# Products of quarters in two shared PSUM tiles: five additions on VectorE for seven, the first quarter read by ScalarE

## The chip, the cores and the metric

The kernel runs on 1 core of a Trainium2 chip. The metric is the device time of one execution in microseconds (us); the median of three runs is the time before. One more execution was taken with the hardware profiler; durations and order of events below come from it.

## The reference

One layer of an encoder block with two parallel mixers, on x of 1024 tokens by 1024 channels, all in float32:

```python
h = rmsnorm(x, norm_gain)
z = jnp.einsum('bsd,de->bse', h, w_in)
q, k, v, gate_a, u_in, v_in, gate_b, g_merge = jnp.split(z, IN_SPLITS, axis=-1)
...
attn = block_attention(q, k, v) * jax.nn.silu(gate_a)
y_a = jnp.einsum('bse,ed->bsd', attn, w_proj_attn)
...
gm = u * v_mix.reshape(B, S, GMLP_WIDTH) * jax.nn.silu(gate_b)
y_b = jnp.einsum('bse,ed->bsd', gm, w_proj_gmlp)
g = jax.nn.sigmoid(g_merge.reshape(B, S, N_BRANCHES, D_MODEL) + b_merge)
y = g[:, :, 0, :] * y_a + g[:, :, 1, :] * y_b
return x + jnp.einsum('bsd,de->bse', y, w_out)
```

A final rmsnorm follows. The change concerns two of these products: g_merge (1024 tokens by 1024 channels by 2 x 1024 columns) and y_a (1024 tokens by 512 by 1024 columns).

## The kernel before

Everything is transposed: channels lie on the 128 partitions, tokens along the free dimension, in two halves of 512 (`H(0)`, `H(1)`). Each float32 operand is split into a high and a low part, and each block product is three matmuls, high by high, high by low, low by high (`mm3`, lines 171 to 174). The stages follow each other: projections of k, v and q, attention (mixed with the other projections), the products for y_b (`proj_b`), then the stage of the change, then the output projection (`out_mm`, tiles out0 to out7) with the residual and the final norm.

In the stage of the change a two by two block product is made from seven products of half-size quarters instead of eight (a Strassen scheme in Winograd's form). `pair(dt, ...)` makes one block row of the gates, ga and gb, for dt of 0 to 7; `proj_pair(i, ...)` makes two block rows of y_a, for i of 0 to 3. Both call `seven`. The sums and differences of the input (forms, written xf for the gates and gf, gk for y_a) are made once in `make_forms`; the sums of the weights in `sums` and line 703. A weight quarter is scaled and cut into its high part on ACT and its low part on DVE (`split16`, lines 680 and 681, tiles wg; `split`, lines 110 and 116, tiles wp). The weights rotate through three buffers, so the parts for a product can be made when the product three before it is done. The seven products are called 11, 21, T2, T3, T1, 22 and T4 by the form that they read. A gate product is 12 matmuls, a projection product 6.

PSUM tiles of the tag "S" are two banks wide (128 x 1024 float32), and there are three of them. Before the change each product takes one and uses its first bank. c is the list of output halves: c[0][0] and c[0][1] are the halves of ga, c[1][0] and c[1][1] those of gb.

`unit_scale` gives the scale of a pair's weights: four squares on ACT (line 814, tiles gsq), a small matmul on PE (usg), a sum on DVE, a power on POOL (scg), a reciprocal on DVE. When a pair and its y_a are ready, `merge` (lines 835 to 837) makes y from them with three 1024-wide instructions, and `split_y` and `out_weight` cut y and the output weights (yhl, who, wo) for the output stage.

The order on each engine is not the order of the code: the scheduler of the tile framework orders instructions by a simulated timeline, with their order in the code as priority, and then sets semaphore waits. Each engine goes through its own list in order, so an instruction that waits holds all that stand behind it. `MORDER` gives the priority of the steps: w0 g0 w1 g1 w2 A a0 g2 w3 g3 w4 a1 g4 and so on, where w is `pair_weights`, g is `pair` and a is `proj_pair`.

Of the kernel before, what the change touches and what calls it, by code (L numbers as in the profile page):

```python
# [12 lines left out]
AF = mybir.ActivationFunctionType  # L13
# [17 lines left out]
def hybrid_block_kernel(  # L31
# [11 lines left out]
    act, dve, pool, pe = nc.scalar, nc.vector, nc.gpsimd, nc.tensor  # L43
# [9 lines left out]
    def t4(tag, name, dt=F32, shape=(P, 1024)):  # L53
        return sb.tile(list(shape), dt, tag=tag, bufs=BUFS[tag], name=name)

    def t2(name, dt=F32):
        return sb.tile([P, 512], dt, tag="t2", bufs=4, name=name)
# [10 lines left out]
    def const(shape, name, dt=F32):  # L68
        return sb.tile(shape, dt, tag=name, bufs=1, name=name)

    def ps_s(name):
        return ps.tile([P, 1024], F32, tag="S", bufs=3, name=name)
# [10 lines left out]
    def H(h):  # L83
        return slice(512 * h, 512 * h + 512)

    def C(c):
        return slice(128 * c, 128 * c + 128)
# [26 lines left out]
    def split(hi, lo, raw, eng, eng_lo=dve):  # L114
        hi_part(eng, hi, raw)
        eng_lo.tensor_tensor(out=lo, in0=raw, in1=hi if hi.dtype == F16 else hi.bitcast(F32), op=ALU.subtract)  # L116

    def load_w(i, half, tag="wraw", bufs=4):
        raw = sb.tile([P, 512], F32, tag=tag, bufs=bufs, name=f"wraw{i}{half}")
        nc.sync.dma_start(out=raw, in_=wall[i, :, H(half)])  # L120
        return raw
# [22 lines left out]
    def load_x(dt):  # L144
        raw = t4("T16", f"xraw{dt}")
        hi = t4("xh", f"xh{dt}", F32R)
        lo = t4("xl", f"xl{dt}", F32R)
        cuts = [slice(0, 256), slice(256, 512), H(1)] if dt == 0 else [slice(0, 1024)]
        for i, r in enumerate(cuts):
            nc.sync.dma_start(out=raw[:, r], in_=xT[C(dt), r])  # L150
            if dt == 0 and i == 0:
                nc.scalar.dma_start(out=cs, in_=cst[:, 0:C_BSP])
            if dt == 0 and i != 1:
                first_w(i // 2)
        for r in cuts:
            act.activation(hi[:, r], raw[:, r], AF.Copy, scale=gain[:, dt:dt + 1])
            dve.scalar_tensor_tensor(out=lo[:, r], in0=raw[:, r], scalar=gain[:, dt:dt + 1], in1=hi[:, r].bitcast(F32),
                                     op0=ALU.mult, op1=ALU.subtract)
        xh.append(hi)
        xl.append(lo)  # L160
        return raw
# [6 lines left out]
        nc.sync.dma_start(out=xn, in_=x[C(tt), :])  # L168
        act.activation(xn, xn, AF.Square, accum_out=ssx[:, tt:tt + 1])

    def mm3(o, ah, al, bh, bl, start, stop):
        pe.matmul(o, ah, bh, start=start, stop=False)  # L172
        pe.matmul(o, ah, bl, start=False, stop=False)  # L173
        pe.matmul(o, al, bh, start=False, stop=stop)  # L174

    kvs = [ps_s(f"kv{b}") for b in range(2)]
    kvb = [s[:, H(h)] for s in kvs for h in range(2)]
    for i in range(4):
        for j in range(2):
            dt = 2 * i + j  # L180
            if dt == 0:
                wh = sb.tile([P, 512], F32R, tag="wh", bufs=3, name="whk0")
                wl = sb.tile([P, 512], F32R, tag="wl", bufs=3, name="wlk0")
                wr = sb.tile([P, 512], F32, tag="wraw", bufs=4, name="wrawk0")
            raw = load_x(dt)
            if i == 0:
                r = slice(256 * j, 256 * j + 256)
                split(wh[:, r], wl[:, r], wr[:, r], act)
            elif j == 0:
                wh, wl = stream_w(W_KV + i // 2, i % 2, act)  # L190
            r = slice(256 * j, 256 * j + 256)
            for tt in range(NT):
                o = kvb[tt // 2][:, 256 * (tt % 2):256 * (tt % 2) + 256]
                mm3(o, xh[dt][:, C(tt)], xl[dt][:, C(tt)], wh[:, r], wl[:, r],
                    dt == 0 and tt % 2 == 0, dt == 7 and tt % 2 == 1)
# [48 lines left out]
    bmh = const([P, 16], "bmh")  # L244
# [10 lines left out]
    for h in range(2):  # L255
        raw = sb.tile([P, 512], F32, tag="wraw", bufs=4, name=f"wspr{h}")
# [37 lines left out]
    def spatial(c, vhl):  # L294
        vh, vl = vhl
        pt = ps_s(f"sp{c}")
        for t in range(4):
            r = slice(256 * t, 256 * t + 256)
            mm3(pt[:, r], vh[:, C(t)], vl[:, C(t)], wsh[:, r], wsl[:, r], True, True)
        p3 = pt.rearrange("p (k i) -> p k i", k=4)  # L300
        for g2 in range(2):
            rows = slice(64 * g2, 64 * g2 + 64)
            act.copy(vm[rows, :, C(c)], p3[rows, :, C(g2)])
# [130 lines left out]
    for t2k in range(4):  # L434
# [5 lines left out]
        for v in range(2):  # L440
            for half in range(2):
                dst = kT[64 * half:64 * half + 64, 2 * v:2 * v + 2, 256 * t2k:256 * t2k + 256]
# [235 lines left out]
    def split16(hi, lo, raw, sc, how):  # L678
        if how == "dve":
            act.activation(hi, raw, AF.Copy, scale=sc[:, 0:1])  # L680
            dve.scalar_tensor_tensor(out=lo, in0=raw, scalar=sc[:, 0:1], in1=hi, op0=ALU.mult, op1=ALU.subtract)
        else:
            act.activation(raw, raw, AF.Copy, scale=sc[:, 0:1])
            split(hi, lo, raw, pool if how == "pool" else act, pool)

    def seven(name, n, w, B, c, weights):

        def product(key, raw):
            hi, lo = weights(key, raw)
            bank = ps_s(f"{name}{key}")[:, H(0)]  # L690
            for j in range(n):
                mm3(bank, hi[:, C(j)], lo[:, C(j)], *B[key][j], j == 0, j == n - 1)
            return bank

        def add(dst, bank, other):
            dve.tensor_tensor(out=dst, in0=bank, in1=other, op=ALU.add)

        a11, a12, a21, a22, s1, s2 = w
        p1 = t2(f"p1{name}")
        act.copy(p1, product("11", a11))  # L700
        add(c[0][0], product("21", a12), p1)
        add(c[0][1], product("T2", s2), p1)
        dve.tensor_tensor(out=s2, in0=a12, in1=s2, op=ALU.subtract)
        add(c[1][0], product("T3", a21), c[0][1])
        o = product("T1", s1)
        add(c[1][1], o, c[1][0])
        add(c[0][1], o, c[0][1])
        add(c[0][1], product("22", s2), c[0][1])
        yield
        add(c[1][0], product("T4", a22), c[1][0])  # L710
        yield

    def sums(a11, a12, a21, a22, s1, s2):
        dve.tensor_tensor(out=s1, in0=a21, in1=a22, op=ALU.add)
        dve.tensor_tensor(out=s2, in0=s1, in1=a11, op=ALU.subtract)
        dve.tensor_tensor(out=a21, in0=a11, in1=a21, op=ALU.subtract)
        return a11, a12, a21, a22, s1, s2
# [63 lines left out]
    for dt in range(8):  # L781
        proj_b(dt)
        if dt in XCS:
            j = XCS.index(dt)
# [4 lines left out]
    def halves_of(t):  # L789
        return [t[:, H(0)], t[:, H(1)]]  # L790

    def proj_pair(i, b, G, dst):
        r0, r1 = load_w(W_PROJ + 2 * i, b), load_w(W_PROJ + 2 * i + 1, b)
        s12 = t2(f"ps{b}{i}")
        w = sums(r0[:, 0:256], r0[:, 256:512], r1[:, 0:256], r1[:, 256:512], s12[:, 0:256], s12[:, 256:512])
        count = [0]

        def weights(key, raw):
            t = sb.tile([P, 2, 256], F32R, tag="wh", bufs=WHB, name=f"wp{b}{i}{key}")
            split(t[:, 0], t[:, 1], raw, act, WPL[count[0] % len(WPL)])  # L800
            count[0] += 1
            return t[:, 0], t[:, 1]

        for _ in seven(f"y{b}{i}", 2, w, G, [halves_of(d) for d in dst], weights):
            pass

    def pair_weights(dt):
        t = t8("qT", 4, f"graw{dt}", F32)
# [9 lines left out]
    def pair(dt, w, sc):  # L818
        def weights(key, raw):
            t = sb.tile([P, 2, 512], F16, tag="wl", bufs=3, name=f"wg{dt}{key}")  # L820
            split16(t[:, 0], t[:, 1], raw, sc, GPW)
            return t[:, 0], t[:, 1]

        ga, gb = (t4(GGT.pop(0), f"g{k}{dt}") for k in "ab")
        it = seven(f"g{dt}", 4, w, XB, [halves_of(ga), halves_of(gb)], weights)
        next(it)
        act.activation(ga, ga, AF.Tanh, bias=bmh[:, dt:dt + 1], scale=sc[:, 1:2])
        next(it)
        act.activation(gb, gb, AF.Tanh, bias=bmh[:, 8 + dt:9 + dt], scale=sc[:, 1:2])
        return ga, gb  # L830

    GGT = GGTAGS.split() * 16
# [49 lines left out]
    for step in MORDER.split():  # L882
        i = int(step[1:] or 0)
# [149 lines left out]
```

## Time and profile before

| | |
|---|---|
| median of 3 runs | 746.56 us (745.75 to 747.24) |
| the profiled execution | 744.79 us, its span 743.0 us |
| PE busy | 712.1 us, 96% of the span |
| DVE busy | 596.4 us, 80% |
| ACT busy | 446.8 us, 60% |
| POOL busy | 97.2 us, 13% |
| PE's granted clock | 0.988 of full speed |

PE is TensorE's matmuls, PEld its weight loads, DVE VectorE, ACT ScalarE, POOL GpSimd, SP the engine that issues most DMAs. A row of a timeline shows start and duration in us, engine, line, operation, output and inputs, and in square brackets how long the engine was idle before it and what ended that. A row of groups shows the number of instructions, their busy time, the mean in ns of one, and the idle time before them. A row of waits shows who waited for whom, the sum in us, how often, and the longest. Matmuls overlap: one of 0.38 us is followed by the next after 0.215.

### The profile page before, as it was taken

What the parts mean: (1) busy time and instruction counts of PE and PEld (TensorE: products, weight loads), DVE (VectorE), ACT (ScalarE), POOL (GpSimd) and SP (SyncE); (2) the same over time, 40 slices, a digit from 0 to 9 for tenths busy, and PEclk for the clock granted to TensorE, in tenths of its full rate; (3) what the DMA queues carried; (4) which work ended last, traced back from release to release, by engine and by line L of the source; (5) the groups of instructions that cost most, each with busy time, mean ns of one, the idle gap of its engine ahead of it and who ended that gap; (6) DMA issues with size and microseconds to landing.
All of it is one profiled execution on the core that took longest, in us unless ns stands there. A gap on an engine that the chain in (4) does not pass through costs nothing.

```text
span 743.0 us, 9814 instructions
## 1 busy us (share of the span) xinstructions
PE 712.1 (96%) x3561; PEld 530.1 (71%) x3561; DVE 596.4 (80%) x931; ACT 446.8 (60%) x775; POOL 97.2 (13%) x77
## 2 busy tenths in 40 slices
PE   8999999988999999999999995999999998999995
PEld 8978888766778888888878882455464555588884
DVE  5568988789798999988899999899888899934223
ACT  6646664676788898768787488555474446611101
POOL 0010242142121321232200002000000000000000
PEclk9999999989999999999999998999999999999998
DMA  8831301083769897898999800130031006241111
GB/s 309 301 100 36 114 15 42 1 142 78 136 128 181 166 179 142 162 177 157 166 234 323 183 16 1 56 128 15 18 125 57 0 1 231 109 142 68 46 58 56
DMA packets 152609, 85.47 MB, mean 115 GB/s; under 512 B 135408, under 2 KB 136048, under 8 KB 152560
## 3 DMA queue, kind: packets, MB, share of 16 engines
q1 hardware_dynamic: 152272, 84.56, 45.7%
q8 instruction: 28, 0.46, 0.3%
q10 hardware_dynamic: 288, 0.28, 0.1%
q14 instruction: 21, 0.17, 0.1%
HBM read 47.07 MB, written 4.19 MB: 69 GB/s over the span
## 4 chain that ended last, share of the span: by engine, by line
PE 81%; DVE 9%; DMA 4%; ACT 2%; issue 2%; POOL 1%; SPq 0%; POOLq 0%; DVEq 0%; ACTq 0%
PE o L575 6%; PE out L174 4%; PE out L173 4%; PE out L172 4%; DMA T<-p 3%; PE s L550 3%; PE s L551 3%; PE g L172 3%; PE g L174 3%; PE g L173 3%; PE q L172 2%; PE q L174 2%; PE v L172 2%; PE q L173 2%; PE v L173 2%; PE v L174 2%
## 5 line engine op out<-in xcount | busy, mean ns | idle before, releaser
L564 DVE SCALAR_TENSOR_TENSOR p<-P,ri,p 128x1024 f16<-128x1024 f32 x64 | 88.9, 1393 | 14.7 <-ACT p L563 14.3
L557 ACT ACTIVATE P<-s,nm 128x1024 f32<-128x1024 f32 x64 | 71.4, 1116 | 23.0 <-DVE nm L553 11.5
L553 DVE TENSOR_REDUCE nm<-s 128x1 f32<-128x1024 f32 x64 | 77.8, 1215 | 5.7 <-PE s L551 5.4
L563 ACT ACTIVATE p<-P,ri 128x1024 f16<-128x1024 f32 x64 | 72.8, 1143 | 14.7 <-DMA T<-p 11.3
L575 PE MATMUL o<-T,vS 128*128 128x256 f16 x512 | 61.8, 273 | 2.1 <-DMA T<-p 2.1
L575 PEld LDWEIGHTS <-vS 128*128 128x128 f16 x512 | 47.4, 98 | 16.0 <-issue 6.9
L550 PE MATMUL s<-kT,qT 128*128 128x512 f32 x128 | 53.0, 414 | 1.3 <-ACT P L557 1.3
L116 POOL TENSOR_TENSOR wl<-wraw,wh 128x512 fp32r<-128x512 f32 x24 | 36.0, 1504 | 111.6 <-ACT wh L110 96.2
L551 PE MATMUL s<-kT,qT 128*128 128x512 f32 x128 | 50.5, 395 | 0.0
L909 ACT ACTIVATE sq<-xr 128x1024 f32<-128x1024 f32 x7 | 7.4, 1061 | 61.5 <-DVE xr L963 61.5
L963 DVE TENSOR_TENSOR xr<-out,xr 128x1024 f32<-128x1024 f32 x7 | 8.6, 1225 | 44.0 <-PE out L174 43.9
L673 POOL TENSOR_TENSOR scg<-scg,mhalf 128x1 f32<-128x1 f32 x8 | 9.8, 1219 | 221.6 <-DVE scg L672 221.6
L110 ACT CAST wh<-wraw 128x512 fp32r<-128x512 f32 x35 | 21.5, 614 | 17.5 <-PE yb L173 7.5
L488 PE MATMUL ga<-xh,wh 128*128 128x512 f32 x64 | 26.5, 414 | 3.8 <-DVE uw L511 3.4
L550 PEld LDWEIGHTS s<-kT,qT 128*128 128x128 f32 x128 | 24.1, 188 | 6.7 <-ACT P L557 1.9
L551 PEld LDWEIGHTS s<-kT,qT 128*128 128x128 f32 x128 | 24.1, 188 | 4.9 <-issue 0.2
L488 PE MATMUL u<-xh,wh 128*128 128x512 f32 x64 | 25.6, 399 | 0.7 <-DVE ga01w L494 0.7
L490 PE MATMUL ga<-xh,wl 128*128 128x512 f32 x64 | 26.1, 407 | 0.0
L489 PE MATMUL ga<-xl,wh 128*128 128x512 f32 x64 | 26.0, 406 | 0.0
L680 ACT ACTIVATE wg<-graw,scg 128x512 f16<-128x512 f32 x16 | 11.4, 721 | 24.2 <-PE g L174 12.8
L172 PE MATMUL v<-nh,xh 128*128 128x512 f32 x64 | 25.5, 398 | 0.0
L174 PE MATMUL yb<-gmh,wl 128*128 128x512 f32 x64 | 25.5, 398 | 0.0
(557 smaller groups left out, 2158.5 us busy)
## 6 DMA issues: line engine op xcount, KB each, us to landing
wraw<-in_wall_dram SPq DMA_DIRECT2D x59, 256.0 KB, 3.2
graw<-in_wall_dram SPq DMA_DIRECT2D x16, 512.0 KB, 4.4
xraw<-in_xT_dram SPq DMA_DIRECT2D x15, 512.0 KB, 7.3
xn<-in_x_dram SPq DMA_DIRECT2D x8, 512.0 KB, 7.6
wor<-in_wall_dram SPq DMA_DIRECT2D x8, 512.0 KB, 4.9
xr<-in_x_dram SPq DMA_DIRECT2D x8, 512.0 KB, 5.1
out_dram<-xr SPq DMA_DIRECT2D x7, 512.0 KB, 2.6
T<-p SPq DMA_TRANSPOSE x64, 4.6
```

The costliest lines, as they stand in the source:

```text
L116: eng_lo.tensor_tensor(out=lo, in0=raw, in1=hi if hi.dtype == F16 else hi.bitcast(F32), op=ALU.subtract)
L172: pe.matmul(o, ah, bh, start=start, stop=False)
L173: pe.matmul(o, ah, bl, start=False, stop=False)
L174: pe.matmul(o, al, bh, start=False, stop=stop)
L488: pe.matmul(o, wh[:, C(dt % 4)], xh[dt][:, H(h)], start=(dt == 0), stop=False)
L550: pe.matmul(sp[:, H(hf)], qs, kT[:, 2 * v, H(hf)], start=True, stop=False)
L551: pe.matmul(sp[:, H(hf)], qs, kT[:, 2 * v + 1, H(hf)], start=False, stop=True)
L553: dve.tensor_reduce(out=nm, in_=sp, axis=AX.X, op=ALU.max, negate=True)
L557: act.activation(Pt, sp, AF.Exp, bias=nm, accum_out=rsum)
L563: act.activation(hi, Pt, AF.Copy, scale=ri)
L564: dve.scalar_tensor_tensor(out=lo, in0=Pt, scalar=ri, in1=hi, op0=ALU.mult, op1=ALU.subtract)
L575: pe.matmul(ot[:, 0:256], vS[:, kt, v, :], T[:, :, 8 * p + kt, :], start=(kt == 0 and p == 0), stop=(kt == 7 and p == 1))
```

## The change

`seven` now takes two PSUM tiles, xy and wz, for all seven products. The four banks are X, Y, W and Z. X takes product 11, is copied, and then takes product 21 on top of it, so that X holds the quarter c[0][0] itself; W takes T3 and later T4 on top, Z takes T1 and later 22. Two of the seven additions of DVE go. The products come in the order 11, T2, T3, 21, T1, T4, 22. The quarter in X is read by ACT: in `pair` by the tanh, which is now done in halves for ga; in `proj_pair` by a copy. The first matmul of a second product doesn't clear its bank; `more` only passes a flag to a check of the framework.

```diff
-    def mm3(o, ah, al, bh, bl, start, stop):
+    def mm3(o, ah, al, bh, bl, start, stop, more=False):
...
     def seven(name, n, w, B, c, weights):
 
-        def product(key, raw):
+
+        xy, wz = ps_s(f"{name}xy"), ps_s(f"{name}wz")
+        X, Y, W, Z = xy[:, H(0)], xy[:, H(1)], wz[:, H(0)], wz[:, H(1)]
+
+        def product(bank, key, raw, first=True):
             hi, lo = weights(key, raw)
-            bank = ps_s(f"{name}{key}")[:, H(0)]
             for j in range(n):
-                mm3(bank, hi[:, C(j)], lo[:, C(j)], *B[key][j], j == 0, j == n - 1)
-            return bank
+                mm3(bank, hi[:, C(j)], lo[:, C(j)], *B[key][j], first and j == 0, j == n - 1, not first)
...
         a11, a12, a21, a22, s1, s2 = w
         p1 = t2(f"p1{name}")
-        act.copy(p1, product("11", a11))
-        add(c[0][0], product("21", a12), p1)
-        add(c[0][1], product("T2", s2), p1)
+        product(X, "11", a11)
+        act.copy(p1, X)
+        product(Y, "T2", s2)
+        add(c[0][1], Y, p1)
         dve.tensor_tensor(out=s2, in0=a12, in1=s2, op=ALU.subtract)
-        add(c[1][0], product("T3", a21), c[0][1])
-        o = product("T1", s1)
-        add(c[1][1], o, c[1][0])
-        add(c[0][1], o, c[0][1])
-        add(c[0][1], product("22", s2), c[0][1])
+        product(W, "T3", a21)
+        add(c[1][0], W, c[0][1])
+        product(X, "21", a12, False)
+        yield X
+        product(Z, "T1", s1)
+        add(c[1][1], Z, c[1][0])
+        product(W, "T4", a22, False)
+        add(c[1][0], W, c[0][1])
         yield
-        add(c[1][0], product("T4", a22), c[1][0])
+        product(Z, "22", s2, False)
+        add(c[0][1], Z, c[0][1])
         yield
...
-        for _ in seven(f"y{b}{i}", 2, w, G, [halves_of(d) for d in dst], weights):
-            pass
+        for bank in seven(f"y{b}{i}", 2, w, G, [halves_of(d) for d in dst], weights):
+            if bank is not None:
+                act.copy(dst[0][:, H(0)], bank)
...
         it = seven(f"g{dt}", 4, w, XB, [halves_of(ga), halves_of(gb)], weights)
+        ba, bb = bmh[:, dt:dt + 1], bmh[:, 8 + dt:9 + dt]
+        act.activation(ga[:, H(0)], next(it), AF.Tanh, bias=ba, scale=sc[:, 1:2])
         next(it)
-        act.activation(ga, ga, AF.Tanh, bias=bmh[:, dt:dt + 1], scale=sc[:, 1:2])
+        act.activation(gb, gb, AF.Tanh, bias=bb, scale=sc[:, 1:2])
         next(it)
-        act.activation(gb, gb, AF.Tanh, bias=bmh[:, 8 + dt:9 + dt], scale=sc[:, 1:2])
+        act.activation(ga[:, H(1)], ga[:, H(1)], AF.Tanh, bias=ba, scale=sc[:, 1:2])
```

The scheduler places the stage's instructions anew on every engine. Up to about 433 us of the profile before, all engines have the same list. In the following lists a name such as g2xy is the tile xy of pair 2, wg221 the weight of its product 21, and "waits" names the engine on whose count the instruction waits. Line numbers after the change are one to fourteen higher.

First PE in pair 2, at the end of product T2. Before:

```order
L174 MATMUL g2T2_5069<-xfT33_4503,wg2T2_5066 128x512
L172 LDWEIGHTS wg2T3_5084 [waits Activation_49]
L172 MATMUL g2T3_5087<-xf110_4250,wg2T3_5084 128x512
L173 LDWEIGHTS wg2T3_5084
L173 MATMUL g2T3_5087<-xf110_4250,wg2T3_5084 128x512
L669 MATMUL usg4_5318<-gss4_5309,mhalf_61 128x4 [waits DVE_49]
```

At the same place after the change, on the same engine:

```order
L175 MATMUL g2xy_5013<-xfT33_4503,wg2T2_5032 128x512
L670 MATMUL usg4_5288<-gss4_5279,mhalf_61 128x4 [waits DVE_49]
L173 LDWEIGHTS wg221_5065 [waits Activation_49]
L173 MATMUL g2xy_5013<-xfT20_4262,wg221_5065 128x512 [waits DVE_49]
L174 LDWEIGHTS wg221_5065
```

Before, T3's first matmul waits for its weights alone; after, product 21 follows T2 at once, and its first matmul has a wait of its own for a count of DVE, which is that of the addition c[0][1] of this pair. The same stands in pairs 0 and 4.

Second DVE around the first addition c[0][1] of pair 0 (output ga0). Before:

```order
L681 SCALAR_TENSOR_TENSOR wg0T3_4658<-graw0_4578,scg0_4592,wg0T3_4658 128x512
L696 TENSOR_TENSOR ga0_4603<-g021_4626,p1g0_4605 128x512
L116 TENSOR_TENSOR xfT31_4321<-xraw5_4212,xfT31_4321 128x512
L716 TENSOR_TENSOR graw1_4729<-graw1_4729 128x512
L681 SCALAR_TENSOR_TENSOR wg0T1_4675<-s10_4598,scg0_4592,wg0T1_4675 128x512
L675 TENSOR_SCALAR scg1_4743<-scg1_4743,gsc_440 128x1
L696 TENSOR_TENSOR ga0_4603<-g0T2_4643,p1g0_4605 128x512
L681 SCALAR_TENSOR_TENSOR wg022_4693<-s20_4599,scg0_4592,wg022_4693 128x512
L116 TENSOR_TENSOR gfT31_4921<-gat0_1919,gfT30_4920 128x1024
```

At the same place after the change, on the same engine:

```order
L722 TENSOR_TENSOR s11_4743<-graw1_4723 128x512
L116 TENSOR_TENSOR xfT31_4321<-xraw5_4212,xfT31_4321 128x512
L682 SCALAR_TENSOR_TENSOR wg021_4657<-graw0_4578,scg0_4592,wg021_4657 128x512
L676 TENSOR_SCALAR scg1_4743<-scg1_4743,gsc_440 128x1
L682 SCALAR_TENSOR_TENSOR wg0T1_4673<-s10_4598,scg0_4592,wg0T1_4673 128x512
L724 TENSOR_TENSOR graw1_4723<-graw1_4723 128x512
L116 TENSOR_TENSOR gfT31_4909<-gat0_1919,gfT30_4908 128x1024
L699 TENSOR_TENSOR ga0_4603<-g0xy_4605,p1g0_4607 128x512
```

The low parts of T1's weights, of the last xfT and of gfT31, one difference and a small instruction stand ahead of the first addition after the change, and behind it before.

Third DVE at pair 7's last additions, where the output stage begins. Before:

```order
L696 TENSOR_TENSOR gb7_6094<-g7T1_6168,gb7_6094 128x512
L696 TENSOR_TENSOR ga7_6093<-g7T1_6168,ga7_6093 128x512
L875 SCALAR_TENSOR_TENSOR yhl2_6226<-y2_4204,yhl2_6226 128x1024
L875 SCALAR_TENSOR_TENSOR yhl4_6240<-y47_4201,yhl4_6240 128x1024
L696 TENSOR_TENSOR ga7_6093<-g722_6186,ga7_6093 128x512
L859 TENSOR_TENSOR wo51_6244<-wor5_6076,wo50_6243 128x1024
L875 SCALAR_TENSOR_TENSOR yhl5_6247<-y47_4201,yhl5_6247 128x1024
L696 TENSOR_TENSOR gb7_6094<-g7T4_6204,gb7_6094 128x512
```

At the same place after the change, on the same engine:

```order
L699 TENSOR_TENSOR gb7_6028<-g7wz_6030,gb7_6028 128x512
L870 TENSOR_TENSOR wo51_6172<-wor5_6010,wo50_6171 128x1024
L870 TENSOR_TENSOR wo61_6179<-wor6_6012,wo60_6178 128x1024
L886 SCALAR_TENSOR_TENSOR yhl4_6168<-y47_4201,yhl4_6168 128x1024
L699 TENSOR_TENSOR gb7_6028<-g7wz_6030,ga7_6027 128x512
L847 SCALAR_TENSOR_TENSOR y47_4201<-gb7_6028,y47_4201 128x1024
L870 TENSOR_TENSOR wo71_6187<-wor7_6014,wo70_6186 128x1024
L886 SCALAR_TENSOR_TENSOR yhl5_6175<-y47_4201,yhl5_6175 128x1024
L699 TENSOR_TENSOR ga7_6027<-g7wz_6030,ga7_6027 128x512
```

Before, two 1024-wide instructions stand ahead of each of the two last additions, and PE has all seven products of pair 7 ahead of the output stage's matmuls; after the change, three 1024-wide instructions of the output weights and of y (wo, yhl) stand between the additions on Z and on W, and three more ahead of the last one, for which product 22 and the tile out2 wait.

More of the change, by code (lines that the diff above doesn't have):

```diff
@@ L169, in add_square @@
         act.activation(xn, xn, AF.Square, accum_out=ssx[:, tt:tt + 1])
-    def mm3(o, ah, al, bh, bl, start, stop):
-        pe.matmul(o, ah, bh, start=start, stop=False)
-        pe.matmul(o, ah, bl, start=False, stop=False)
-        pe.matmul(o, al, bh, start=False, stop=stop)
+    def mm3(o, ah, al, bh, bl, start, stop, more=False):
+        pe.matmul(o, ah, bh, start=start, stop=False, skip_group_check=more)
+        pe.matmul(o, ah, bl, start=False, stop=False, skip_group_check=more)
+        pe.matmul(o, al, bh, start=False, stop=stop, skip_group_check=more)
     kvs = [ps_s(f"kv{b}") for b in range(2)]
```

## The prediction

> **What bounds the kernel now.** I read the page's first lines, then the table by stretches, then what PE waited for, since PE is busy almost all the time.
>
> ```profile
> span 743.0 us, 9814 instructions
> PE 712.1 (96%) x3561; PEld 530.1 (71%) x3561; DVE 596.4 (80%) x931; ACT 446.8 (60%) x775; POOL 97.2 (13%) x77
> ```
> ```profile
> core 0: us, PE busy (x) PEld busy (x) DVE busy (x) ACT busy (x) POOL busy (x), PEclk, DMA share, GB/s
> 448.00:468.00 20.00, 11.47 (x44) 4.82 (x45) 19.10 (x33) 14.93 (x27) 6.08 (x2) 0.83 0.00 1
> 470.00:617.00 147.00, 147.00 (x682) 78.35 (x681) 128.85 (x223) 77.66 (x139) 3.68 (x6) 1.00 0.15 51
> 617.00:632.00 15.00, 12.81 (x55) 8.45 (x54) 14.82 (x20) 9.50 (x15) 0.00 (x0) 1.00 0.80 299
> ```
> ```profile
> PE usg L669 <- ACT gsq L814: 6.8, 2, 5.7
> PE g0T L174 <- DVE wg0T L681: 1.6, 1, 1.6
> PE y03T L174 <- DVE wp03T L116: 1.5, 1, 1.5
> PE g L172 <- ACT wg L680: 0.8, 1, 0.8
> PE y L174 <- DVE wp L116: 0.6, 1, 0.6
> ```
>
> The stage of the products of quarters runs from 448 to about 650 us. From 470 to 617 us PE is busy for 147.00 of 147.00 us, while DVE has 128.85: PE is the bound, and an addition taken from DVE there is worth nothing. PE idles only at the entry (448 to 468, 8.5 us) and at the exit (617 to 632, 2.2 us, of which 1.5 and 0.6 are waits for DVE). So DVE's relief can win 2.1 us at the exit, and perhaps the 1.6 us of the entry. Anything that makes PE wait between 470 and 617 is a full loss.
>
> **The units.** These rows give the prices: a product's matmuls, what follows its end, and DVE's and ACT's instructions.
>
> ```profile
> 611.11 0.69 DVE L696 TENSOR_TENSOR gb<-g6T,gb 128x512 f32<-128x512 f32 x1 [0.20 <-PE g6T L174]
> 611.72 0.68 DVE L696 TENSOR_TENSOR ga<-g6T,ga 128x512 f32<-128x512 f32 x1
> 613.29 0.38 PE L174 MATMUL g<-xfT,wg 128*128 128x512 f16 x1
> 613.50 0.38 PE L172 MATMUL g6T<-xfT,wg6T 128*128 128x512 f16 x1
> 613.70 0.69 DVE L696 TENSOR_TENSOR ga<-g,ga 128x512 f32<-128x512 f32 x1 [0.31 <-PE g L174]
> 614.43 1.24 ACT L827 ACTIVATE ga<-ga,bmh,scg 128x1024 f32<-128x1024 f32 x1
> ```
> ```profile
> 496.26 0.39 PE L174 MATMUL y<-gf,wp 128*128 128x512 f32 x1
> 496.49 0.40 PE L172 MATMUL y<-gf,wp 128*128 128x512 f32 x1
> ```
> ```profile
> 651.50 1.22 DVE L836 SCALAR_TENSOR_TENSOR y<-gb,y 128x1024 f32<-128x1024 f32 x1
> 652.64 1.22 DVE L859 TENSOR_TENSOR wo<-wor,wo 128x1024 fp32r<-128x1024 f32 x1
> ```
> ```profile
> L681 DVE SCALAR_TENSOR_TENSOR wg<-graw,scg,wg 128x512 f16<-128x512 f32 x13 | 9.7, 746 | 0.6
> L814 ACT ACTIVATE gsq<-graw 128x512 f32<-128x512 f32 x24 | 14.3, 596 | 0.3
> L680 ACT ACTIVATE wg<-graw,scg 128x512 f16<-128x512 f32 x12 | 8.7, 722 | 20.3 <-PE g L174 11.0 <-PE g4T L174 1.9 <-PE g2T L174 1.9
> L814 ACT ACTIVATION_READ_ACCUMULATOR gsq<-graw 128x1 f32 x24 | 4.5, 186 | 0.0
> L700 ACT COPY p1g<-g 128x512 f32<-128x512 f32 x6 | 3.5, 583 | 5.1 <-PE g L174 5.1
> L673 POOL TENSOR_TENSOR scg<-scg,mhalf 128x1 f32<-128x1 f32 x6 | 3.7, 613 | 137.1 <-DVE scg L672 137.1
> ```
>
> A gate product is 12 matmuls, one each 0.215 us: 2.6 us; a projection product 6 at 0.23: 1.4 us. Back to back, DVE needs 0.61 us for a 512-wide addition and 1.14 for a 1024-wide instruction. The last matmul of a product begins at 613.29, its slot ends at 613.50, the addition begins at 613.70 and ends at 614.39. So a product that waits for an addition on the product just before it starts 0.9 us after that one's slot, with DVE free.
>
> **What the change removes and adds.** Each of 12 calls of `seven` loses two DVE additions: 24 x 0.61 = 14.6 us of DVE work. 147 us of the stage have PE full, so this is hidden but for the exit's 2.1 us. ACT gains 12 instructions: four copies, 4 x 0.58, and eight more tanh, since halves replace whole tiles; two halves cost at most 2 x 0.72 for 1.24. ACT has 69 us idle of the 147 from 470 to 617, which cover that. PE's matmuls are the same in number, and DMAs too; the two loads of xr that SP issues earlier are wanted after 650 us, so that costs nothing. The flag for the check has no instruction.
>
> What it adds is waits. Before, each product had its own two-bank tile of three, so a product waited for an addition three products back. Now X with Y, and W with Z, are halves of one tile, and the built program makes the waits by tile: product 21 waits for the count that c[0][1] (the addition on Y) reaches, T1 for c[1][0], T4 for c[1][1], 22 for c[1][0]'s second, and T2 for ACT's copy of X. That is a chain through DVE's queue, and DVE is in order: all that stands ahead of the addition counts. The scheduler fills gaps with other pairs' products only where one is ready. I follow the places where the order puts nothing between.
>
> *Entry, pair 0.* The rows before:
>
> ```profile
> 455.90 0.61 PE L172 MATMUL g<-xf,wg 128*128 128x512 f16 x1 [0.82 <-ACT wg L680]
> 456.30 0.63 PE L173 MATMUL g<-xf,wg 128*128 128x512 f16 x1
> 459.34 0.38 PE L173 MATMUL g<-xfT,wg 128*128 128x512 f16 x1
> 459.55 0.38 PE L174 MATMUL g<-xfT,wg 128*128 128x512 f16 x1
> 460.24 0.74 DVE L681 SCALAR_TENSOR_TENSOR wg0T<-s,scg,wg0T 128x512 f16<-128x512 f32 x1
> 460.40 4.54 POOL L673 TENSOR_TENSOR scg<-scg,mhalf 128x1 f32<-128x1 f32 x1 [5.32 <-DVE scg L672]
> 460.90 0.68 DVE L116 TENSOR_TENSOR xfT<-xraw,xfT 128x512 f16<-128x512 f32 x1
> 467.45 0.68 DVE L696 TENSOR_TENSOR ga<-g,p1g 128x512 f32<-128x512 f32 x1
> 467.58 0.39 PE L174 MATMUL g0T<-xf,wg0T 128*128 128x512 f16 x1 [1.61 <-DVE wg0T L681]
> ```
>
> Before, DVE's first addition begins at 467.45, and at 467.58 PE goes on with its 39th matmul of pair 0. Now PE does 11, T3 and T2 (36 matmuls, to about 465.7) and stops at 21. Ahead of c[0][1] DVE has, more than before, the low parts of T1's weights (0.66, from 460.24 to 460.90), of one xfT (0.61) and of gfT31 (1.14), one difference (0.61) and a small one (0.1): 3.1 us; a 256-wide one, half of 0.61, has gone behind. So it begins near 470.2 and PE goes on at 471.0, with two matmuls fewer done: 3.4 + 0.4 = 3.8 us behind. Four products later, usg2 waits for two of ACT's squares (0.78 each with their readout) that now stand behind the tanh of X and a weight: 021's end at 473.7, then 2 x 0.72 and 2 x 0.78, 476.7, where PE was ready at 476.1; c[1][1] then frees T4 at 477.1. With usg2's own time, which was there before, taken off, that is 0.7 us. Entry: 4.5.
>
> *Pairs 2 and 4.* The row is T2, usg, 21: nothing between. From the end of y00's T4, PE has 11, T3, T2 (3 x 2.6), one projection product (1.4) and two small ones (0.5): 9.7 us. DVE has up to c[0][1]: four 1024-wide (4.6), seven 512-wide (4.4, two of them low parts at 0.66), small ones (0.3), c[0][1] itself (0.7), and POOL's power with both handovers (0.7), for which it now stands still, as nothing is between: 10.7 us. ACT holds it 0.9 us more: four squares, a copy and a tanh stand ahead of the high part of 21's weights. That makes 11.6, and with the 0.2 of the product's end and 0.1 to start 21, 11.9 against 9.7: 2.2 us. Then T4 comes straight behind T1: 0.9. In all 3.1 for each, 6.2. The odd pairs have projection products between, and each addition there ends 1 to 3 us ahead of the product that waits: nothing.
>
> *Pair 6* has y03's first product (1.4) between T2 and 21 and no squares on ACT: 0.4.
>
> *Exit, pair 7.* The first products of the output stage fill in up to T4. Behind T4 comes 22 at once, and it waits for c[1][0]'s second addition; ahead of that DVE has three 1024-wide parts of the output stage, the first of them held by T4's own third matmul (its buffer): 0.8 + 3 x 1.14 + 0.7 = 4.9 us after T4's start, where T4 lasts 2.6: 2.3. Then out2 needs the tile of W and Z: its last addition stands behind the tanh of gb (1.24) and three 1024-wide ones, 1.24 + 3.4 + 0.7 = 5.3 us, against 2.6 of product 22: 2.7. Together 5.0.
>
> **The sum.** 4.5 + 6.2 + 0.4 + 5.0 - 2.1 (the exit's old waits, whose DVE work is now shifted) = 14.0 us. The profiled execution took 744.79 us for its span of 743.0, 1.8 under the median of the runs, 746.56; 744.8 becomes 758.8, and the median 760.6.
>
> The low ends: pairs 2 and 4 can't cost less than two bare waits each (1.8), pair 6 nothing, the exit one bare 0.9 and half of the rest (2.5), the entry 3.0 if ACT's squares come in time and POOL is quick (it took 4.54 us once, 0.61 in the mean later): 7.0, so 753.6. The high ends: 4 for each even pair if POOL is slow once more, pair 6 1.4, exit 6, entry 6: 19.3, so 766. I take the worked values, since they are nearest to rows of this stage.
>
> **A rule on the banks.** The Trainium skill, "PSUM — Partial Sum Buffer", section "PSUM bank collisions raise a hardware error", asks for a guard by bank and quadrant, so a product into X would not have to wait for a reading of Y. What that would give is rival 2; the waits in the built program speak against it.
>
> **The rivals.** 1: DVE's relief wins. Place: product 21 of pair 0. If c[0][1] there ended before T2 does (465.7, that is 5.2 us sooner than I work out) and the even pairs' within 9.7 us, PE would see no new wait, and the 1.6 of the entry and the 2.1 of the exit would go: 746.6 - 3.7 = 742.9. For it speaks DVE's 14.6 us less; against it that DVE is busy for 19.10 of 20 us at the entry, with work that is not additions.
>
> 2: waits by bank. 21 then waits for weights alone, T1 for nothing, T4 for c[1][0]: the even pairs cost nothing, the entry about 0.8 us, while out2 still waits for the last addition (5.0): 746.6 + 0.8 + 5.0 - 2.1 = 750.3.
>
> 3: the clock falls at the entry. After the idle of 5.7 us PE's matmuls begin 0.40 apart (455.90, 456.30) and reach 0.21 at 459.34: seven at 0.2 more, 1.4 us. The new stop of 5.2 us is near that one; the one of 1.61 at 467.58 had no such tail. It would give 762.0. The Trainium skill, "TensorE: Matmul & The Clock Gate", part 1, says that an idle window of about 3.4 us halves the clock; a stop of 5.2 would hold one or not, as the windows run free. The trace agrees as far as it goes.
>
> **The numbers.** Forecast 0.74, rival 3 0.10, rival 2 0.06, rival 1 0.06, and 0.04 for no change by some balance of these. Below 0.2% (1.5 us) a measurement of this kernel can't tell a change from none. Slower: 0.74 + 0.10 + 0.06 = 0.90; same 0.04; faster 0.06. The range goes from 751, between rival 2 and the low ends, to 766, the high ends.
>
> **What would show it.** In the profile after, PE should be idle some 10 us between 465 and 617 us, where it was idle 2; what PE waited for should name DVE's additions (line 699), first at 21 of pairs 0, 2 and 4 with about 5, 2 and 2 us, and T4 of pairs 2 and 4 with 0.9; near the end at 22 of pair 7 and at out2 with 2 to 3 us each. DVE's busy time should fall by some 15 us. If PE stays full there, the forecast is wrong by its waits; if PE's stops are twice as long, by DVE's queue.

## The result and the profile after

The changed kernel takes 764.14 us (median of 4 runs, 763.26 to 766.51) against 746.16 us for the kernel before on the same chip (4 runs, 745.75 to 747.24). The ratio is 1.0256, 95% interval 1.0236 to 1.0277: slower by 18.0 us. The forecast was 760.6 us, range 751 to 766. The sign, the time and most places were right; one cost of some 7 us was missing, and terms that were priced too high stood in for about half of it.

The profiled execution after took 766.51 us. First its busy times, then the stage of the change in stretches (columns as before the change: busy time of PE, weight loads, DVE, ACT and POOL, then the clock granted to PE).

```profile
span 764.7 us, 9777 instructions
PE 721.5 (94%) x3561; PEld 531.3 (69%) x3561; DVE 586.7 (77%) x907; ACT 449.2 (59%) x787; POOL 96.6 (13%) x77
```

```profile
468.00:480.00 12.00, 7.41 (x27) 2.79 (x25) 7.50 (x13) 4.97 (x12) 0.00 (x0) 0.86 0.23 87
480.00:617.00 137.00, 131.52 (x589) 68.54 (x590) 101.38 (x171) 68.53 (x128) 3.18 (x5) 0.98 0.13 47
```

Before, PE was busy for all of the 147 us from 470 to 617 at a clock of 1.00. Now it has gaps in both stretches, and the clock is below 1 in both. What PE waited for in the stage at DVE's additions, in us in all, times, and the longest:

```profile
PE g0xy L173 <- DVE ga L699: 4.3, 1, 4.3
PE g7wz L173 <- DVE gb L699: 2.4, 1, 2.4
PE g4xy L173 <- DVE ga L699: 1.9, 1, 1.9
PE g2xy L173 <- DVE ga L699: 1.9, 1, 1.9
PE out L173 <- DVE ga L699: 1.4, 1, 1.4
PE g4wz L173 <- DVE gb L699: 0.8, 1, 0.8
PE g2wz L173 <- DVE gb L699: 0.8, 1, 0.8
PE g6xy L173 <- DVE ga L699: 0.6, 1, 0.6
```

All are new and all name DVE's additions (line 699); behind the old waits for ACT at the entry there are two more short ones for weights, 0.4 and 0.2 us in pair 0. The eight stand where the forecast put them: 21 of pairs 0, 2, 4 and 6, T4 of pairs 2 and 4, 22 of pair 7, out2. With 0.26 us at usg2 they are 14.4 us. Before, PE waited 1.6, 1.5 and 0.6 us for other things there, and these waits are gone; so 10.6 us are stops.

The rest is the clock. These are PE's rows around product 21 of pair 2; one row is one matmul, with its start and duration.

```profile
521.32 0.38 PE L175 MATMUL g2xy<-xfT,wg2T 128*128 128x512 f16 x1
521.53 0.28 PE L670 MATMUL usg<-gss,mhalf 128*128 128x4 f32 x2
523.70 0.38 PE L173 MATMUL g2xy<-xfT,wg 128*128 128x512 f16 x1 [1.89 <-DVE ga L699]
...
524.13 0.60 PE L175 MATMUL g2xy<-xfT,wg 128*128 128x512 f16 x1
524.52 0.63 PE L173 MATMUL g2xy<-xfT,wg 128*128 128x512 f16 x1
...
527.98 0.38 PE L173 MATMUL g2wz<-xf,wg2T 128*128 128x512 f16 x1
531.51 0.38 PE L173 MATMUL g2wz<-xfT,wg2T 128*128 128x512 f16 x1 [0.78 <-DVE gb L699]
531.73 0.38 PE L174 MATMUL g2wz<-xfT,wg2T 128*128 128x512 f16 x1
```

Two matmuls after the stop the rows lengthen to 0.60 and 0.63 and come 0.43 apart instead of 0.215. Product 21 takes from 523.70 to 527.98, 4.28 us instead of 2.58. Behind the stop of 0.78 at 531.51 nothing of the kind is seen. The granted clock shows the same:

```profile
520.74:524.15 3.41, 1.52 (x10) 0.83 (x9) 3.41 (x6) 0.72 (x1) 0.00 (x0) 1.00 0.00 0
524.15:527.56 3.41, 3.41 (x10) 1.21 (x9) 1.27 (x5) 0.00 (x0) 0.55 (x1) 0.50 0.00 0
```

In the first of these rows PE stands still for 1.9 us and the clock is 1.00; the fall to half comes after the stop and lasts 3.41 us. It follows the stops of 4.3, 1.9, 1.9 and 2.4 us, each time for about eight matmuls, 1.7 us: 6.8 in all. 10.6 + 6.8 = 17.4 us. These are figures of the profiled execution. It was the slowest of the four and took 20.3 us longer than the one before from the first usg to its end, where the medians differ by 18.0. Of the other 2.9 us, 0.6 are the two short waits for weights in pair 0, and 0.9 come ahead of the first stop, where the clock stays at half up to 462.71, for eleven matmuls of pair 0, while the kernel before has eight at half; the last 1.4 are not traced.

### The profile page after: what moved, and what is told of

It reads as the page before. It is cut to its first block, busy times and chain, and to the rows that moved or that the text cites. A ratio compares the mean times of both kernels' runs of the same rounds, so it can differ in the third digit from the quotient of the medians.

```text
span 764.7 us, 9777 instructions
## 1 busy us (share of the span) xinstructions
PE 721.5 (94%) x3561; PEld 531.3 (69%) x3561; DVE 586.7 (77%) x907; ACT 449.2 (59%) x787; POOL 96.6 (13%) x77
## 4 chain that ended last, share of the span: by engine, by line
PE 76%; DVE 14%; DMA 4%; ACT 3%; issue 2%; POOL 1%; SPq 0%; POOLq 0%; DVEq 0%; ACTq 0%
PE o L576 5%; PE out L173 4%; PE out L175 4%; PE out L174 4%; DMA T<-p 3%; PE s L551 3%; PE s L552 3%; PE q L173 2%; PE q L175 2%; PE v L174 2%; PE v L173 2%; PE v L175 2%; PE q L174 2%; PE gb L491 2%; PE gb L489 2%
## 5 line engine op out<-in xcount | busy, mean ns | idle before, releaser
L174 PEld LDWEIGHTS <-wg 128*128 128x128 f16 x96 | 10.1, 106 | 23.3 <-issue 15.4
L173 PE MATMUL yb<-gmh,wh 128*128 128x512 f32 x64 | 25.2, 396 | 0.5 <-ACT gmh L110 0.5
```

Source lines behind the costliest of these rows:

```text
L173: pe.matmul(o, ah, bh, start=start, stop=False, skip_group_check=more)
L174: pe.matmul(o, ah, bl, start=False, stop=False, skip_group_check=more)
```

## The experiments

Theory A, after this reading: the built program's waits are by PSUM tile; the stops follow from them, and behind a stop of about 2 us or more the clock falls. The rivals are that the waits come with the order and the additions whatever the tile, that the reading by ACT costs, that the matmuls are slow for another reason, and that DVE's load matters by itself.

**1. Three tiles instead of two.** Only the layout of the four banks is changed.

```diff
-        xy, wz = ps_s(f"{name}xy"), ps_s(f"{name}wz")
-        X, Y, W, Z = xy[:, H(0)], xy[:, H(1)], wz[:, H(0)], wz[:, H(1)]
+        xx, yz, ww = (ps_s(f"{name}{k}") for k in ("x", "yz", "w"))
+        X, Y, W, Z = xx[:, H(0)], yz[:, H(0)], ww[:, H(0)], yz[:, H(1)]
```

> The changed kernel with its four banks laid on three PSUM tiles instead of two: X alone in the first, Y and Z as the halves of the second, W alone in the third. Same products in the same order of the code, same five additions, same reads by ACT, nothing left out. Product 21 then waits for ACT's copy of X alone, T1 for the first addition on Y, T4 for the first on W. Theory A (the loss is waits by tile, and the falls of the clock that follow the stops): the stops of 4.3, 1.9 and 1.9 us at product 21 and those at T4 go, and with them the slow matmuls, 11 + 8 us of the 20 found between the profiles; 744 to 750 us. Theory B (the waits come from the order 11, T2, T3, 21, T1, T4, 22 and the additions on the way, whichever tile the banks lie in): 758 us or more. Theory C (the price is the reading by ACT and the tanh in halves): 764 us, as the changed kernel.

Measured: 744.96 us (10 runs, 741.23 to 746.68), ratio to before 0.9983, interval 0.9965 to 1.0002. The whole loss is gone, with the five additions, the order of the code and the reads by ACT as they were, so neither the order of the code (theory B) nor ACT's reads (theory C) can be its cause. Since this did not say whether the kernel beats the one before, it was measured once more.

> The kernel with three tiles for a call once more, in five rounds, since 0.9983 [0.9965, 1.0002] did not say whether it is faster than before. Theory A: 0.997 to 0.999, faster by 1 to 2 us, from the exit's old waits. Rival: no difference, the interval lies on both sides of 1.

Measured: 744.33 us (10 runs, 742.43 to 745.68) against 745.95, ratio 0.9977, interval 0.9963 to 0.999: faster by 1.6 us. This is the version that beats both. What PE waited for in this second profile, besides the old waits for ACT at the entry, and its main stretch:

```profile
PE g0x L175 <- DVE wg L682: 1.4, 1, 1.4
PE y03yz L173 <- DVE ya L699: 0.4, 1, 0.4
PE g0yz L173 <- DVE ga L699: 0.3, 1, 0.3
PE g0w L173 <- DVE gb L699: 0.2, 1, 0.2
```
```profile
480.00:617.00 137.00, 137.00 (x634) 73.54 (x632) 110.42 (x192) 72.91 (x137) 4.57 (x6) 1.00 0.15 54
```

Of 14.1 us of stops at additions 0.9 is left, and PE is full from 480 to 617 at a clock of 1.00. The scheduler's list on PE changes with the tiles: 21 now stands ahead of T3. But in pair 2 it still follows T2 directly (T2 from 510.3 us, the rest of 21 from 512.9), two of its matmuls even run ahead of T2, and PE does not stop: X shares no tile with Y any more.

**2. The stops filled.** Matmuls of no use behind T3, ahead of W's addition in the code:

```diff
         product(W, "T3", a21)
+        fill(Z, "T3", FILL.get(name, 0))
         add(c[1][0], W, c[0][1])
...
+    FILL = {"g0": 20, "g2": 9, "g4": 9}
```

> The changed kernel with matmuls of no use put into bank Z behind T3 in pairs 0, 2 and 4 (20, 9 and 9 of 128x512 in f16, 8.2 us of PE in all), so that PE is busy where it stood still for 4.33, 1.89 and 1.89 us ahead of product 21; T1 clears the bank afterwards. The output is the same. Theory A (a stop of 1.9 us or more makes the clock fall, so that eight matmuls come 0.42 apart): no slow matmuls behind product 21 of these pairs, 3 x 1.7 = 5.1 us less than the changed kernel's 764.1, so 759, though PE has 8.2 us more of work. Rival (the matmuls are slow for another reason, or the waits alone make the loss): 764 to 767 us, with the slow matmuls still there or the time taken by the added ones.

Measured: 761.74 us (4 runs, 759.98 to 763.85), 2.4 less than the changed kernel; the intervals of the two ratios to before (1.0178 to 1.0236 here) just touch. The clock, and PE's rows at 21 of pair 2 and at pair 7, in the profile of this kernel:

```profile
524.00:528.00 4.00, 4.00 (x20) 1.82 (x19) 2.62 (x8) 1.49 (x3) 0.55 (x1) 1.00 0.00 0
```
```profile
523.32 0.38 PE L173 MATMUL g2xy<-xfT,wg 128*128 128x512 f16 x1
...
525.90 0.38 PE L173 MATMUL g2wz<-xf,wg2T 128*128 128x512 f16 x1
667.19 0.38 PE L173 MATMUL g7wz<-xf,wg 128*128 128x512 f16 x1 [2.43 <-DVE gb L699]
...
672.59 0.50 PE L173 MATMUL out<-who,yhl 128*128 128x512 f32 x1 [2.65 <-DVE ga L699]
```

Product 21 now takes 523.32 to 525.90, 2.58 us: with PE busy the clock stays, and 1.7 us are won at pair 2 and at pair 4. That the stops cause the falls is shown. The expected 5.1 us did not come out whole. At the entry the added matmuls fill the stop a little more than full, and the clock is at half for longer ahead of it (to 465.34 us, 8.9 us from the start of the second usg, where the changed kernel has 6.8), so T4 of pair 0 comes only 0.85 us sooner, counted from the first usg. At the exit 1.25 are given back: 22 of pair 7, after a stop of the same 2.43 us as in the changed kernel, now runs at full clock, so out2 waits 2.65 for the last addition instead of 1.40, and the clock falls behind that stop instead (run 5 shows both). 0.85 + 1.7 + 1.7 - 1.25 = 3.0, where the medians differ by 2.4.

**3. DVE's relief without the shared banks.** The kernel before, less two additions a call, so that two quarters lack a term; ACT reads product 21 from its bank:

```diff
-        add(c[0][0], product("21", a12), p1)
+        yield product("21", a12)
...
-        add(c[0][1], o, c[0][1])
...
```

> The kernel before, with its seven tiles and its order of products, and two additions of DVE for each call left out: that of p1 to product 21 (ACT reads product 21 from its bank, the tanh of ga in halves, as in the changed kernel) and that of T1 to c[0][1]. So the quarters c[0][0] and c[0][1] lack a term each; DVE has the load of the changed kernel and PE waits by product as before. Theory A (PE is the bound in this stage, DVE's relief is worth nothing but the old waits of 1.6 us at the entry and 2.1 at the exit): 743 to 746.5. Theory C (the reading by ACT in halves costs): over 748. Rival 1 of the prediction in full: 742.9.

Measured: 742.34 us (4 runs, 742.09 to 745.62), ratio 0.9945, interval 0.9925 to 0.9964: 3.6 us faster by the medians, just below what was expected of theory A and 0.6 under the figure of rival 1. What PE waited for in its profile:

```profile
PE g0T L174 <- DVE wg0T L681: 1.1, 1, 1.1
PE y L174 <- DVE wp L116: 0.8, 1, 0.8
```

Against 1.6 at the entry and 1.5 + 0.6 at the exit, 1.8 us are accounted for. Counted from the first usg to PE's last matmul, this execution takes 284.9 us and the one before 286.9, so 2.0 us is what the profile shows of the relief. The rest of the 3.6 is not shown to come from the change: the profiled run was the slowest of its four (745.62, the others 742.1 to 742.4) and reached the first usg 2.8 us later than the one before, ahead of the stage that was changed. The reading by ACT in halves costs nothing that shows.

**4. Which pair of banks.** First X and Y alone as halves of one tile, then W and Z alone:

```diff
+        xy, ww, zz = (ps_s(f"{name}{k}") for k in ("xy", "w", "z"))
+        X, Y, W, Z = xy[:, H(0)], xy[:, H(1)], ww[:, H(0)], zz[:, H(0)]
```
```diff
+        xx, yy, wz = (ps_s(f"{name}{k}") for k in ("x", "y", "wz"))
+        X, Y, W, Z = xx[:, H(0)], yy[:, H(0)], wz[:, H(0)], wz[:, H(1)]
```

> The changed kernel with only X and Y as halves of one PSUM tile; W and Z lie in tiles of their own. Nothing left out. Product 21 still waits for the first addition c[0][1], but T1 no longer waits for W's addition and stands ahead of 21 in PE's list, so 21 is asked for 2.6 us later; T4 waits for c[1][0] and 22 for c[1][1], each with a product between. Theory A (each stop is a wait by tile less the work that PE has before it): the stop at 21 of pair 0 is 4.3 - 2.6 = 1.7 us, those of pairs 2 and 4 (1.9) and at T4 (0.8) are gone, and the slow matmuls of pairs 2, 4 and 7 too: 746 to 750 us. Rival (the loss belongs to 21's wait for the addition on Y, as such): 755 us or more.

> The changed kernel with only W and Z as halves of one PSUM tile; X and Y lie in tiles of their own. Nothing left out. 21 waits for ACT's copy alone; T1 waits for c[1][0], T4 for c[1][1], 22 for the second c[1][0], out2 for the last addition, as in the changed kernel. Theory A: the entry's stop moves from 21 to T1 and shrinks to 2 to 4 us, T4's 0.8 of each even pair may stay, and the exit's 2.4 + 1.4 with its slow matmuls (1.7) stays: 750 to 756 us, more than with X and Y shared. Rival (the loss belongs to X and Y): 744 to 748 us.

Measured: X and Y shared 745.2 us (10 runs), ratio 0.9989, interval 0.9973 to 1.0004; W and Z shared 760.33 us (4 runs), ratio 1.0203, interval 1.0169 to 1.0237. With X and Y shared PE waits at no addition; its longest new stop is 1.5 us at the entry, for the weights of T1. With W and Z shared:

```profile
PE g0wz L173 <- DVE gb L699: 3.8, 2, 3.2
PE g7wz L173 <- DVE gb L699: 2.4, 1, 2.4
PE g4wz L173 <- DVE gb L699: 1.6, 1, 1.6
PE g2wz L173 <- DVE gb L699: 1.6, 1, 1.6
PE out L173 <- DVE ga L699: 1.0, 1, 1.0
```

So 14.3 of the 18.0 us come with W and Z in one tile, and nothing with X and Y alone. In the first kernel the scheduler puts T1 of the gates between T2 and 21, since Z is free, and 21's wait for Y's addition is over when PE comes to it. With W and Z in one tile T1 has to wait for W's addition, PE has nothing to put there, and it stands still ahead of T1, or, in the changed kernel, ahead of 21. The two waits do not add up. The expected 750 to 756 for W and Z was 4 to 10 too low: I had left out the 1.6 us of pairs 2 and 4 at T1, 0.9 in each of pairs 3 and 5 for a weight from ACT, and the fall of the clock behind the 3.2.

**5. Stops of many lengths by themselves.** Two kernels with 60 bursts of matmuls, after each of which DVE reads the bank:

> Another kernel altogether: 60 bursts of 41 to 57 matmuls (128x512, f16, about 9 to 12 us each) on two banks, and behind each burst DVE reads the banks in 256 to 4608 columns, for which the next burst waits; so 15 lengths of stop from about 0.7 to 6 us, four of each in mixed order. It computes nothing of the reference. Theory A (length alone decides, between 1.61 and 1.89 us): no matmul at 0.42 behind stops up to 1.6 us, about eight behind each stop over 1.9. Theory B (a window of some 3.4 us that runs free, in which half must be idle): the same below 1.7 and over 3.4 us, and between them both kinds, more slow ones the longer the stop. Rule of a whole idle window of 3.4 us (the Trainium skill, TensorE: Matmul & The Clock Gate, part 1): slow matmuls behind no stop under 3.4 us, behind some up to 6.8.

> Another kernel altogether, as the one with 15 lengths of stop, with 60 stops of five lengths from about 1.6 to 2.2 us, twelve of each, and a small matmul (128x4, as usg) at the end of each burst. It computes nothing of the reference. Among the earlier stops none of 12 from 1.64 to 1.91 us had slow matmuls and 1 of 4 of 2.04, though in the changed kernel both of 1.89 had. Theory A (windows of about 3.4 us that run free and an edge at some 0.57 of one, in which the time of the small matmul counts as idle nearly in full): some of the stops shown as 1.77 to 1.9 have about eight slow matmuls, those of 1.64 none, and the share grows with length. Rival (length alone, and in the changed kernel something else makes it): none under 2.0.

Rows of the first (start, duration of the burst, number of its matmuls, the stop ahead of it), then of the second:

```profile
29.22 12.85 PE L53 MATMUL bank<-xf 128*128 128x512 f16 x51 [2.04 <-DVE res L57]
456.55 11.60 PE L53 MATMUL bank<-xf 128*128 128x512 f16 x53 [2.04 <-DVE res L57]
```
```profile
30.43 11.17 PE L53 MATMUL bank<-xf 128*128 128x512 f16 x51 [1.91 <-DVE res L58]
687.68 12.85 PE L53 MATMUL bank<-xf 128*128 128x512 f16 x51 [2.18 <-DVE res L58]
```

The same 51 matmuls take 11.17 us behind one stop and 12.85 behind another: 1.7 more. By length, stops with such a tail: none of 63 up to 1.91 us; 5 of 16 at 2.04; 4 of 15 at 2.17 or 2.18; 2 of 8 from 2.31 to 2.58; 3 of 4 at 3.03; all 12 from 3.56 on, where the tail is up to 2.9. So there is an edge near 2.0 us, and above it length alone does not decide. In the changed kernel the rows of pair 2 show it: T2's last full matmul is at an end at 521.70 (521.32 + 0.38) and 21 begins at 523.70, 2.00 us, since usg is only a small matmul. The profile calls it 1.89. Both expectations of theory A were off: length alone does not decide above the edge, and no stop shown as 1.77 to 1.91 had a tail, as the rival of the second had it. Theory B of the first, windows that run free, came nearest.

The traces hold more than lengths. The granted clock changes only at the edges of windows of 3.41 us, which follow each other in one fixed grid through each trace. So for each window one can ask how long PE was idle in it, with the small matmuls of 128x4 not counted as work, and whether the next window ran at half clock. In the twelve traces of this case, without the first 20 us of each, where some windows do not follow, and without windows that were at half clock already, PE was idle for 2.01 us or more in 57 windows, and the clock halved behind every one of them; it was idle for 1.96 us or less in 2426, 94 of them over 1.2, and the clock halved behind none. Of the two between, one at 1.97 had a fall behind it and one at 1.99 had none. So what decides is the idle time within one window, with an edge at 2.0 us. The windows around pair 7 show it, first in the changed kernel, then in that of run 2:

```profile
667.51:670.92 3.41, 1.09 (x6) 0.39 (x4) 3.32 (x4) 1.94 (x2) 0.00 (x0) 1.00 0.00 0
670.92:674.34 3.42, 3.31 (x8) 1.17 (x8) 1.83 (x3) 2.30 (x2) 0.00 (x0) 0.50 0.00 0
```
```profile
663.31:666.72 3.41, 1.45 (x7) 0.58 (x6) 3.32 (x4) 2.11 (x2) 0.00 (x0) 1.00 0.00 0
666.72:670.14 3.42, 2.75 (x12) 1.07 (x11) 2.11 (x3) 2.19 (x2) 0.00 (x0) 1.00 0.02 5
670.14:673.55 3.41, 0.96 (x4) 0.82 (x5) 2.52 (x4) 0.82 (x1) 0.00 (x0) 1.00 0.40 154
673.55:676.96 3.41, 3.41 (x10) 2.64 (x9) 3.38 (x3) 2.08 (x2) 0.00 (x0) 0.50 0.00 0
```

In the changed kernel 2.3 of the 2.43 us lie in one window, and the next is at half clock. In run 2 an edge of the grid cuts the same stop into 1.96 and 0.47, and nothing falls; there the stop ahead of out2 has 2.45 us in one window, and the fall comes behind it. Pairs 2 and 4 behave alike since their stops are 51.0 us apart, close to 15 windows; each has 2.01 us in one window, just over the edge. With usg counted as work it would be 1.9, less than in windows without a fall. How a program lies to the grid is chance, so another execution of the same kernel may have fewer falls than this one.

The Trainium skill, "TensorE: Matmul & The Clock Gate", part 1, says that the activity is watched in windows of 4096 cycles, 3.41 us, that run free, and that the clock halves after an idle window. The windows agree with the traces; that a whole one has to be idle does not: 2.0 us of it are enough.

**6. What DVE's load is worth with three tiles.** Two of the five additions done twice, so that DVE has seven again:

```diff
         add(c[0][1], Y, p1)
+        add(c[0][1], Y, p1)
...
         add(c[1][1], Z, c[1][0])
+        add(c[1][1], Z, c[1][0])
```

> The kernel with three tiles for a call (X; Y and Z; W), and two of its five additions done twice over (c[0][1] on Y, c[1][1] on Z; the second gives the same numbers), so that DVE has seven additions a call again, 24 x 0.61 = 14.6 us more. Nothing left out. Theory A (PE is the bound from 480 to 617 us, so DVE's relief is worth only what it takes out of the entry and the exit, some 1 to 2 us): 745.5 to 748 us. Rival (DVE's load counts in the whole stage): 752 us or more.

Measured: 750.4 us (5 runs, 749.51 to 750.65), 6.1 more than three tiles alone, over theory A's range and under the rival's. From the profile, its main stretch, then the two waits of PE that differ most:

```profile
480.00:617.00 137.00, 137.00 (x634) 73.50 (x633) 119.14 (x204) 73.69 (x134) 4.55 (x6) 1.00 0.13 48
```
```profile
PE g0yz L173 <- DVE ga L699: 3.2, 1, 3.2
PE g7x L175 <- DVE wg L682: 1.3, 1, 1.3
```

From 480 to 617 us PE is full with 8.7 us more of DVE's work: there DVE's load is worth nothing, as forecast. The loss lies at the ends. DVE's rows at the entry say how:

```profile
470.08 0.68 DVE L699 TENSOR_TENSOR ga<-g0yz,p1g 128x512 f32<-128x512 f32 x1
...
473.08 0.68 DVE L699 TENSOR_TENSOR ga<-g0yz,p1g 128x512 f32<-128x512 f32 x1
```

The repeated addition on Y came to stand 3.0 us behind the first, and T1 waits for it: 3.2 us for 0.3, with a fall of the clock behind it (some 1.7). Pair 7 waits 1.3 more for its weights. 2.9 + 1.7 + 1.3 - 0.4 (a wait in y03 that is gone) = 5.5 us, where the medians differ by 6.1 and the two profiled executions by 5.6 from the first usg on. So most of this is the place of one addition in DVE's list and not DVE's load, and the kernel is no clean measure of the load at the ends.

**7. An attempt to shorten the entry.** Two differences of the forms of y_a moved to POOL, with three tiles:

```diff
-    ASUB = (dve, dve, dve, dve)
+    ASUB = (dve, dve, pool, pool)
```

> The kernel with three tiles for a call (X; Y and Z; W), and two of the four 1024-wide differences of the projection's forms (gat) moved from DVE to POOL. They stand in DVE's list ahead of the low part of product 21's weights in pair 0, for which PE waited 1.9 us there. Nothing left out. Theory A (PE waits at the entry for DVE's list as a whole): 2 x 1.14 = 2.3 us less ahead of it, the stop of 1.9 goes or shrinks under 0.5: 742 to 744 us. Rival (POOL needs 1.4 us for 512 columns, so 2.8 for each difference, and the forms then come late, or the two engines hold each other up): 745 to 748 us.

Measured: 747.03 us (10 runs, 744.47 to 749.5), ratio 1.0021, interval 1.0001 to 1.0041: slower than three tiles by 2 to 3 us. PE's stop in 21 of pair 0, for the weights, grew from 1.4 to 4.0 us. POOL's and DVE's rows at that time:

```profile
455.95 2.73 POOL L653 TENSOR_TENSOR gat<-gat,gat 128x1024 f32<-128x1024 f32 x1 [1.46 <-DVE scg L672]
458.75 2.68 POOL L653 TENSOR_TENSOR gat<-gat 128x1024 f32<-128x1024 f32 x1
```
```profile
456.39 2.83 DVE L653 TENSOR_TENSOR xraw<-xraw,xraw 128x512 f32<-128x512 f32 x1
459.27 2.70 DVE L682 SCALAR_TENSOR_TENSOR wg<-graw,scg,wg 128x512 f16<-128x512 f32 x1
461.90 0.74 DVE L682 SCALAR_TENSOR_TENSOR wg0T<-s,scg,wg0T 128x512 f16<-128x512 f32 x1
```

Each of POOL's two held one of DVE's: 2.83 and 2.70 us for what takes 0.68 and 0.74 alone, and both times DVE's row ends 0.54 us after POOL's (459.22 and 458.68, 461.97 and 461.43). The rival is right, by its second half.

## Why the prediction was right, and where it was not

- *What bounds the kernel.* Right: PE, with DVE's relief worth nothing while PE is full (run 6). At the two ends I gave it 2.1 us; without the shared banks the profile shows 2.0 and the medians 3.6 (run 3).
- *Entry, 4.5.* The stop was 4.33 us where I had 5.2, because PE came to 21 later (0.6 for two waits for weights, 0.9 for matmuls at half clock); it went on at 472.69, or at 471.3 if the 1.4 us by which this execution reached the stage later are taken off, against 471.0. DVE's list ahead of c[0][1] was read rightly. usg2 stopped PE for 0.26.
- *Pairs 2 and 4, 2.2 + 0.9 each.* Measured 1.9 + 0.8.
- *Pair 6, 0.4.* Measured 0.6.
- *Exit, 2.3 + 2.7.* Measured 2.4 + 1.4. The 2.7 was right for a product 22 at full clock, as run 2 shows (2.65).
- *The old waits, 2.1.* Gone, as said. DVE's busy time fell by 9.7 us where I had 15. Added up by their own durations DVE's instructions fell by 15.3, from 651.1 to 635.8: 24 additions of 0.68 are gone, 16.2, and all others together grew by 0.9. The busy time counts once what overlaps, and DVE's rows overlap less now, by 49.1 us instead of 54.7. So the 15 was right, and the busy time the wrong sign to look for.
- *The step that failed* is the clock. It stood in the prediction as rival 3 with a chance of 0.10, a price of 1.4, and for the entry alone, because the stop of 1.61 had no tail and I had no row between 1.61 and 5.7. The price was misread too: between 455.90 and 459.34 there are eight matmuls, not seven, and they take 3.44 us instead of 1.72, so the price is 1.7. It was 1.7 at four places, 6.8 us in all. The waits came out 3.4 below the sum (10.6 for 14.0), and the two errors partly cancelled: 14.0 forecast, 18.0 measured. That is luck: the sum as it stood with 6.8 more gives 767.4, outside the range. In its time, 762.0, rival 3 came nearer than the forecast, and at the entry the clock fell as it said.
- *The cause* was named too narrowly. I put the even pairs' loss on X and Y in one tile; alone that costs nothing (run 4). It needs W and Z in one tile as well, which keeps T1 behind W's addition and leaves PE nothing to do ahead of 21.
- *Rival 2*, waits by bank, did not hold for this program, but its idea did: with tiles laid so that waits fall on additions that are long done, the same additions and reads take 744.3 us, 6 below the 750.3 that I gave it, since out2's wait goes too.

## What to carry to other kernels

Where waits are kept by tile, choose which halves share one by asking what may still run while the other half is read: the same four banks cost 18 us on two tiles and won 1.6 on three. Price a stop of the matmul engine with its tail: here 2.0 us of idle time in one window of 3.41 us cost 1.7 more, so two stops of 0.8 are cheaper than one of 2.0. Work taken from an engine that is not the bound is worth only what it removes from the chain at the ends of a stage.

## What the hardware showed that I had not expected

The clock fell behind stops that the profile calls 1.89 us, with the full matmuls 2.00 apart; in the two kernels of stops none of 63 up to 1.91 us did it and 5 of 16 at 2.04 did. The reason is a grid of windows of 3.41 us: 2.01 us of idle time or more in one of them halved the clock in the next in 57 of 57 cases, up to 1.96 us in none of 2426. The loss is about 1.7 us for one slow window, and up to 2.9 behind longer stops. And a 1024-wide difference on POOL (2.7 us) held a 512-wide instruction of DVE until it was done, so that it took 2.83 us for 0.68; the Trainium skill, "GPSIMD Engine Reference", section "1. Specifications", says that the two share their way to SBUF and contend where DVE has two inputs there, and these rows agree.
